# The next block's output product taken ahead of the last channel group of a feed-forward, with the residual sums passed through DRAM

## The chip, the cores and the metric

One NeuronCore of a Trainium2 chip. The metric is the device time of one execution in microseconds, given as the median of several runs.

## The reference

One layer of a decoder trunk over 2048 tokens of width 1024, in float32:

```python
h = rmsnorm(x, norm1_g) * (1 + sc1) + sh1
p = h @ w_in                                   # 27 columns of 128 channels
y = concat([rglru(...), hgrn2(...), rwkv7(...)]) * mix_beta   # three recurrent mixers over the tokens
x = x + g1 * (y @ w_out)
h = rmsnorm(x, norm2_g) * (1 + sc2) + sh2
x = x + g2 * ((silu(h @ w_gate) * (h @ w_up)) @ w_down)       # 2816 channels
return rmsnorm(x, final_g)
```

The six shift, scale and gate vectors come from a conditioning vector. The mixers carry a state from token to token; everything else works on each token alone.

## The kernel before

All tensors lie transposed, channels on the 128 partitions and tokens along the free axis. The tokens are cut into NB = 4 blocks of TB = 512, the width into KC = 8 pieces of 128, the feed-forward channels into NF = 22 groups of 128. So a block of x is eight tiles of 128x512.

Every projection runs in `project`: for each piece of the contraction three matmuls of 128x512, since both operands are split into a rounded part and a remainder (`hh`, `hl` of the activations, `wh`, `wl` of the weights): `hh` by `wh`, `hl` by `wh`, `hh` by `wl`. One product of a whole contraction of 1024 is 24 matmuls into one PSUM bank of the pool `pd`, which has three. A weight tile comes by a DMA of SyncE into a buffer `wr` (three of them), ScalarE rounds it to `wh` and VectorE forms `wl` (four of each). The pools `hh` and `hl` have 16 tiles each, the pool `xs` of plain float32 tiles 12.

A block b goes through these steps:

- `load_y(b)`: eight loads from the DRAM tensor `yd`, into which the mixers wrote, and their splits.
- `w_out_products(b)`: eight products of 24 matmuls. Each bank is evicted by one VectorE instruction (`stt`) that multiplies by the gate and adds to the tile of x; squares are summed on the side.
- `rstd_of`: the sums over the channels by four matmuls (L358 to L361), then logarithm and exponential on ScalarE. `make_h` (norm2) follows: for each of eight pieces a VectorE product with rstd (`xs<-xs,Q,rstd`), a ScalarE rounding (`hh<-xs,Q`) and a VectorE remainder (`hl<-xs,Q,hh`).
- `ffn(b)`: for each of the 22 channel groups two products of 24 matmuls (`ffn_up`); after every fourth group the eight products with `w_down` over those four groups (12 matmuls each, the last time over two groups, 6 matmuls each). Each is evicted by an `stt` that adds it to the tiles of x. So the groups go 4, 4, 4, 4, 4, 2. `load_y(b+1)` stands ahead of the w_down products of the last 4.
- `final_norm`: another `rstd_of` and eight `stt`, then the stores to `out`. For block b it stands behind the first product of `w_out_products(b+1)`.

Ahead of all this come the products with `w_in` for all blocks, whose results go to a DRAM tensor `pd` (stores of L1012). For the blocks 2 and 3 the last NT = 5 columns are done at the end, block 2 first, then block 3, then `load_y(0)`.

The mixers of all blocks are traced in small steps in between (`tick`, `step`, `finish`), so their instructions lie between the matmuls of the projections until they have done all four blocks.

What sets the order: a scheduler orders the instructions of each engine ahead of the run, by readiness in its own estimate and by a priority, which `level` sets. Lowest numbers go first: "out" (evictions) ahead of everything, then plain loads, "feed", "mix", and "dense" last. On the chip each engine runs its list in that order. SyncE's list holds nearly all DMAs; an entry that waits holds up those behind it.

Line 69 is the line of a wrapper through which all VectorE and ScalarE instructions go, so groups are told apart by their operands. L155 is the load of a weight tile, L164 that of any other tile, L267 the matmuls of `project`, L298 and L303 those of the mixers.

Of the kernel before, what the change touches and what calls it, by code (L numbers as in the profile page):

```python
# [10 lines left out]
F = mybir.dt.float32  # L11
# [3 lines left out]
OP = mybir.AluOpType  # L15
PSUM = bass.MemoryType.PSUM

T = 2048
D = 1024
FF = 2816  # L20
TB = 512
KC = D // 128
NB = T // TB
NF = FF // 128
# [11 lines left out]
IN_ORDER = (25, 26, 19, 16, 20, 17, 22, 23, 7, 4, 10, 13, 0, 2, 21, 18, 24, 8, 5, 11, 14, 1, 3, 9, 6, 12, 15)  # L36
# [38 lines left out]
def hybrid_kernel(ctx, tc, x, par, ada_w, w_in, rgw, igw, w_up, a_up, g_up, w_out,  # L75
                  w_gate, w_upf, w_down, cst, msk, out):
    nc = tc.nc
    G, PE, SP = nc.gpsimd, nc.tensor, nc.sync
# [3 lines left out]
    dp = ctx.enter_context(tc.tile_pool(name="dp", bufs=1))  # L82
# [7 lines left out]
    @contextmanager  # L90
    def level(name):

        clock[levels[-1]] = tc.cur_priority
        levels.append(name)
        tc.cur_priority = clock[name]
        yield
        clock[name] = tc.cur_priority
        levels.pop()
        tc.cur_priority = clock[levels[-1]]
# [4 lines left out]
    def stt(o, a, s, b, op0, op1):  # L104
        return V.scalar_tensor_tensor(o, a, s, b, op0=op0, op1=op1)
# [38 lines left out]
    def pc(name, i=0):  # L144
        a, b = PCOLS[name]
        assert a + i < b
        return P[:, a + i:a + i + 1]
# [98 lines left out]
    def load_w(src, fn):  # L246
        ws = []
        with level("load"):
            for c in range(0, src.shape[1], TB):
                n = min(TB, src.shape[1] - c)  # L250
                w = raw_w(src[:, c:c + n])
                hi, lo = w_parts()
                fn(w[:, :n], hi[:, :n], lo[:, :n])
                ws.append((hi, lo))
        return ws

    def project(h, *cols):

        ps = [bank("pd", 3) for ws in cols]
        tot = 3 * len(h)  # L260
        with level("dense"):
            for k, (hh, hl) in enumerate(h):
                c = slice((k % 4) * 128, (k % 4 + 1) * 128)
                for p, ws in zip(ps, cols):
                    wh, wl = ws[k // 4]
                    for n, (a, b) in enumerate(((wh, hh), (wh, hl), (wl, hh)), 3 * k):
                        PE.matmul(p, a[:, c], b, start=(n == 0), stop=(n == tot - 1))  # L267
                    now[0] += 0.68
                if k % (4 // len(ps)) == 4 // len(ps) - 1 or k == len(h) - 1:
                    tick()  # L270
        return ps
# [61 lines left out]
    def square_sum(s, t, k, tile=None, n=1):  # L333

        s, *last = s or (None,)
        if len(last) == n:
            if s is None:
                s = last.pop(0)
            else:
                V.tensor_add(s, s, last.pop(0))  # L340
        q = (tile or xs_)()
        if k == KC - 1:
            V.tensor_mul(q, t, t)
        else:
            squared[:] = [act(q, t, AF.Square)]
        return s, *last, q
# [18 lines left out]
    def load_x(src, b, k, tile=None):  # L365
        t = (tile or xs_)()
        load(t, src[k, :, b * TB:(b + 1) * TB])
        return t
# [15 lines left out]
    def make_h(xt, rs, gain, shift, table=None, ks=range(KC), over=True):  # L384

        hs = []

        def low(k, t, hi, lo):
            stt(lo, t, shift[:, k:k + 1], hi.bitcast(F), OP.add, OP.subtract)
            hs.append((hi, lo))  # L390

        todo = []
        for k in ks:
            x_ = xt(k)
            t = x_ if over else xs_()
            stt(t, x_, gain[:, k:k + 1], rs, OP.mult, OP.mult)
            hi, lo = parts_()
            i = act(hi, t, AF.Identity, bias=shift[:, k:k + 1])
            todo.append((k, t, hi, lo))
            if len(todo) > 2:  # L400
                low(*todo.pop(0))
        for a in todo:
            low(*a)
        if table is not None:
            order(A.preload_act_table_set(table), i)
        return hs

    def drain(it):
        for _ in it:
            pass  # L410
# [586 lines left out]
    def w_in_products(h, cols, side):  # L997

        n = 0
        while n < len(cols):  # L1000

            cs_ = cols[n:n + 2] if n == 0 and len(h) == 1 else cols[n:n + 1]
            ws = [W.pop(c) if c in W else load_w(w_in[c], split_v) for c in cs_]
            for i, b in enumerate(h):
                for j, (c, p) in enumerate(zip(cs_, project(h[b], *ws))):
                    with level("feed"):
                        t = xs_()
                        if (n + i + j) % 2:
                            act(t, p)
                        else:  # L1010
                            V.tensor_copy(t, p)
                        SP.dma_start(pd[c, :, b * TB:(b + 1) * TB], t)  # L1012
                        stored.add((c, b))
                    next(side, None)
            n += len(cs_)
# [24 lines left out]
    def load_y(b):  # L1040
        finish(b)
        ys = []
        for k in range(KC):
            t = load_x(yd, b, k)
            y = parts_()
            split_v(t, *y)
            ys.append(y)
        return ys

    def w_out_products(b, ys, before):  # L1050
        x1, s = [], None
        for d in range(KC):
            ws = load_w(w_out[d], split_v)
            t = load_x(x, b, d)
            p, = project(ys, ws)
            with level("out"):
                stt(t, p, G1[:, d:d + 1], t, OP.mult, OP.add)
            if d == 0:
                before()
            s = square_sum(s, t, d)  # L1060
            x1.append(t)
        return x1, rstd_of(s)

    def ffn_up(h, f):
        if f:
            p, = project(h, load_w(w_gate[f], split_v))
        else:
            p, pu = project(h, load_w(w_gate[f], split_v), load_w(w_upf[f], split_v))
        t = xs_()
        with level("out"):  # L1070
            act(t, p, AF.Silu)
        if f:
            pu, = project(h, load_w(w_upf[f], split_v))
        with level("out"):
            V.tensor_mul(t, pu, t)
        g = parts_()
        split_v(t, *g)
        return g

    def ffn(b, x1, rs):  # L1080
        h = make_h(lambda k: x1[k], rs, A2, B2, "silu_and_others", over=False)
        gs, s, ys = [], None, None
        for f0 in range(0, NF, 4):
            n = min(4, NF - f0)
            while len(gs) < min(f0 + n + (2 if f0 + n + 2 >= NF else 1), NF):
                gs.append(ffn_up(h, len(gs)))
            if len(gs) == NF and ys is None and b + 1 < NB:
                ys = load_y(b + 1)
            for d in range(KC):
                p, = project(gs[f0:f0 + n], load_w(w_down[d][:, f0 * 128:(f0 + n) * 128], split_v))  # L1090
                with level("out"):
                    stt(x1[d], p, G2[:, d:d + 1], x1[d], OP.mult, OP.add)
                if f0 + n == NF:
                    s = square_sum(s, x1[d], d, n=1 if b + 1 < NB else 2)

        def final_norm():
            rs = rstd_of(s)
            for d in range(KC):
                with level("dense"):
                    stt(x1[d], x1[d], pc("final_g", d), rs, OP.mult, OP.mult)  # L1100
                    SP.dma_start(out[d, :, b * TB:(b + 1) * TB], x1[d])

        return ys, final_norm

    side = ada_rest()
    NH, NT = 4, 5
    for b0 in range(0, NB, 2):
        h = {b0: h0}
        if b0 + 1 < NB:
            head, rest = IN_ORDER[:NH], IN_ORDER[NH:-NT]  # L1110
            w_in_products(h, head, ahead)
            drain(ahead)
            h1 = {b0 + 1: norm1(b0 + 1)}
            w_in_products(h1, head, side)
            h.update(h1)
            ahead = x_stats(range(b0 + 2, min(b0 + 4, NB)), 1)
            w_in_products(h, rest, chain(islice(side, 16), ahead, side))
            drain(ahead)
            w_in_products({b0: h[b0]}, IN_ORDER[-NT:], side)
            if b0 + 2 < NB:  # L1120
                h0 = norm1(b0 + 2)
            w_in_products(h1, IN_ORDER[-NT:], side)
        else:
            w_in_products(h, IN_ORDER, side)
    drain(side)
    with level("feed"):
        ys, before = load_y(0), lambda: None
    for b in range(NB):
        with level("feed"):
            ys, before = ffn(b, *w_out_products(b, ys, before))  # L1130
    before()


# [54 lines left out]
```

## Time and profile before

| | |
|---|---|
| Median of 3 runs | 2843.93 us (2843.27 to 2844.93) |
| The profiled execution: time, span | 2842.49 us, 2840.7 us |
| Mean granted TensorE clock | 0.989 |
| TensorE busy | 2724.8 us, 96% of the span |
| VectorE busy | 1934.6 us, 68% |
| ScalarE busy | 1472.7 us, 52% |
| DMA engines, mean | 124 GB/s, 352.27 MB moved |

The span runs from the first to the last instruction of the profiled execution; 1.8 us lie around it. In rows of groups the names of buffers stand without numbers, the count behind an x, the busy time in us, the mean time of one in ns, and after the second bar the idle time of the engine just before such instructions and what ended most of it.

### The profile page before, as it was taken

The numbers are of one execution on the slowest core, as the hardware profiler recorded it, in microseconds if no ns is written. First come the engines' busy times: TensorE is split into PE (matmuls) and PEld (weight loads), VectorE is DVE, ScalarE is ACT, GpSimd is POOL, SyncE is SP. The second block draws the span as 40 slices with busy tenths as digits, with TensorE's granted clock in tenths as the row PEclk, the third lists the DMA queues.
The fourth block names the chain that finished last, engine by engine and source line by source line (L and its number), as shares of the span: only waits on it lengthen the run. The fifth ranks groups of instructions, "written<-read, shape, count | busy, mean of one in ns | idle before, by whom it ended". The sixth has DMA issues, their size and how long they took to land. (4 is left out here: it accounts for less than half of the span.)

```text
span 2840.7 us, 41245 instructions
## 1 busy us (share of the span) xinstructions
PE 2724.8 (96%) x14842; PEld 2188.8 (77%) x14842; DVE 1934.6 (68%) x4150; ACT 1472.7 (52%) x2464; POOL 26.5 (1%) x29
## 2 busy tenths in 40 slices
PE   7999998999999999999999999999999999999998
PEld 6777776777877788877777877877777788788886
DVE  7668667866686785687887767788786445644445
ACT  5433854454647743666487546655863433533333
POOL 1000000000000000000000000000000000000000
PEclk9999999999999999999999999999999999999999
DMA  7553455544444242434533424335233334433332
GB/s 259 179 156 115 132 169 163 160 133 149 128 127 142 84 123 85 133 106 128 154 93 101 119 83 136 111 118 160 82 103 106 89 97 119 146 97 98 97 97 86
DMA packets 242588, 352.27 MB, mean 124 GB/s; under 512 B 72912, under 2 KB 78544, under 8 KB 242384
## 3 DMA queue, kind: packets, MB, share of 16 engines
q1 hardware_dynamic: 160144, 285.55, 32.4%
q10 hardware_dynamic: 82240, 64.09, 8.5%
q8 instruction: 117, 1.92, 0.3%
q14 instruction: 87, 0.71, 0.1%
HBM read 293.92 MB, written 55.62 MB: 123 GB/s over the span
## 5 line engine op out<-in xcount | busy, mean ns | idle before, releaser
L267 PE MATMUL pd<-hh,wh 128*128 128x512 f32 x3232 | 1289.5, 400 | 20.6 <-ACT hh L69 19.2
L267 PE MATMUL pd<-hl,wh 128*128 128x512 f32 x3232 | 1280.8, 396 | 3.8 <-DVE hl L69 3.7
L267 PE MATMUL pd<-hh,wl 128*128 128x512 f32 x3232 | 1281.9, 397 | 0.0
L69 ACT ACTIVATE wh<-wr 128x512 fp32r<-128x512 f32 (+1 forms) x752 | 463.8, 620 | 879.4 <-PE pd L267 692.9
L267 PEld LDWEIGHTS pd<-hh,wh 128*128 128x128 f32 x3232 | 612.2, 190 | 150.0 <-ACT hh L69 21.9
L267 PEld LDWEIGHTS pd<-hl,wh 128*128 128x128 f32 x3232 | 612.3, 189 | 133.8 <-DVE hl L69 9.1
L267 PEld LDWEIGHTS pd<-hh,wl 128*128 128x128 f32 x3232 | 611.8, 189 | 127.9 <-issue 3.4
L69 DVE TENSOR_TENSOR wl<-wr,wh 128x512 fp32r<-128x512 f32 (+1 forms) x752 | 504.2, 674 | 301.1 <-ACT wh L69 284.2
L69 ACT ACT_TABLE_LOAD x225 | 288.7, 1283 | 12.0 <-DVE th L69 4.5
L69 DVE SCALAR_TENSOR_TENSOR xs<-pd,Q,xs 128x512 f32<-128x512 f32 x224 | 167.6, 748 | 131.5 <-PE pd L267 123.5
L69 DVE TENSOR_TENSOR th<-th 128x256 f32<-128x256 f32 (+7 forms) x355 | 158.0, 458 | 26.8 <-ACT th L69 23.4
L69 ACT ACTIVATE th<-th 128x512 f32<-128x512 f32 (+2 forms) x153 | 93.5, 612 | 47.5 <-DVE th L69 22.8
L69 DVE TENSOR_TENSOR big<-big 128x30 f32<-128x30 f32 (+7 forms) x480 | 108.2, 225 | 10.1 <-DMA big<-nd 0.2
L69 DVE TENSOR_TENSOR xs<-pd,xs 128x512 f32<-128x512 f32 x88 | 60.6, 689 | 76.8 <-PE pd L267 74.2
L69 ACT ACTIVATE xs<-pd 128x512 f32<-128x512 f32 x140 | 82.6, 590 | 57.0 <-PE pd L267 53.0
L69 ACT ACTIVATE hh<-xs 128x512 fp32r<-128x512 f32 x120 | 74.4, 628 | 39.8 <-DVE xs L69 25.0
L69 DVE TENSOR_TENSOR hl<-xs,hh 128x512 fp32r<-128x512 f32 x120 | 81.7, 688 | 14.1 <-ACT hh L69 9.8
L69 ACT ACTIVATE hw<-big,we 64x64 f32<-64x64 f32 x192 | 66.2, 345 | 37.9 <-DVE big L69 31.6
L69 ACT ACTIVATE tr<-tr 128x512 fp32r<-128x512 f32 (+4 forms) x112 | 69.5, 627 | 17.5 <-DVE tr L69 16.3
L69 ACT ACTIVATE xs<-xs 128x512 f32<-128x512 f32 x77 | 48.1, 627 | 43.6 <-DVE xs L69 40.1
L69 DVE SCALAR_TENSOR_TENSOR big<-pc,we,hw 64x64 f32<-64x64 f32 x168 | 47.5, 283 | 30.8 <-PE pc L298 28.1
L69 DVE TENSOR_TENSOR tr<-tr 128x512 fp32r<-128x512 f32 (+2 forms) x80 | 54.7, 686 | 19.1 <-ACT tr L69 18.5
(183 smaller groups left out, 2220.4 us busy)
## 6 DMA issues: line engine op xcount, KB each, us to landing
wr<-in_w_gate SPq DMA_DIRECT2D x176, 256.0 KB, 2.6
wr<-in_w_upf SPq DMA_DIRECT2D x176, 256.0 KB, 2.6
wr<-in_w_down SPq DMA_DIRECT2D x160, 256.0 KB, 2.7
wr<-in_w_in SPq DMA_DIRECT2D x144, 256.0 KB, 3.3
pd<-xs SPq DMA_DIRECT2D x108, 256.0 KB, 3.1
xs<-in_x SPq DMA_DIRECT2D x72, 256.0 KB, 4.3
wr<-in_ada_w SPq DMA_DIRECT2D x64, 256.0 KB, 3.2
th<-pd ACTq DMA_DIRECT2D x64, 256.0 KB, 3.5
```

The source lines that it names most:

```text
L69: return f(*a, **k)
L267: PE.matmul(p, a[:, c], b, start=(n == 0), stop=(n == tot - 1))
```

## The change

Four things, all in the order of the work. The matmuls, evictions and splits stay as many as they were.

1. The groups of a feed-forward go 2, 4, 4, 4, 4, 4.
2. `ffn` does all groups but the last. Then `load_y(b+1)`, `w_out_products(b+1)` and norm2 of b+1 follow, and only then `ffn_last(b)`, the w_down products of the last four groups of block b.
3. Two blocks' sums are alive at once, and the pool `xs` has no room for both. So in the fifth group the tiles of block b are stored to a DRAM tensor `xr`; `ffn_last` loads them into tiles of the pools `hh` and `hl` (`spare`), adds its products and stores them to `xf`; `final_norm` loads them from `xf`, again into such tiles, and stands behind the channel groups 0 to 2 of the next feed-forward. Block 3 does without this.
4. The five last w_in columns of block 3 (5 products of 24 matmuls) go from ahead of `load_y(0)` to behind norm2 of block 0.

So there are 96 more DMAs of 256 KB: for each of three blocks 8 stores to `xr`, 8 loads from it, 8 stores to `xf`, 8 loads from it.

```diff
-    def ffn(b, x1, rs):
-        h = make_h(lambda k: x1[k], rs, A2, B2, "silu_and_others", over=False)
...
+    GROUPS = (2, 4, 4, 4, 4, 4)
+    def ffn_down(gs, f0, d):
+        p, = project(gs, load_w(w_down[d][:, f0 * 128:(f0 + len(gs)) * 128], split_v))
+        return p
+    def norm2(x1, rs):
+        return make_h(lambda k: x1[k], rs, A2, B2, "silu_and_others", over=False)
+    def ffn(b, x1, h, before):
+        gs, f0 = [], 0
+        for i, n in enumerate(GROUPS[:-1]):
+            while len(gs) < min(f0 + n + 1, NF):
+                gs.append(ffn_up(h, len(gs)))
+            if i == 0:
+                before()
+            if i == len(GROUPS) - 2:
+                while len(gs) < NF:
+                    gs.append(ffn_up(h, len(gs)))
             for d in range(KC):
+                p = ffn_down(gs[f0:f0 + n], f0, d)
                 with level("out"):
                     stt(x1[d], p, G2[:, d:d + 1], x1[d], OP.mult, OP.add)
+                    if b + 1 < NB and i == len(GROUPS) - 2:
+                        SP.dma_start(xr[d, :, b * TB:(b + 1) * TB], x1[d])
+            f0 += n
+        return gs[f0:], f0
+    def spare(i):
+        return dp.tile([128, TB], F, name="hl" if i % 2 else "hh", bufs=16)
+    def ffn_last(b, x1, gs, f0):
+        s, ts_ = None, []
+        for d in range(KC):
+            t = load_x(xr, b, d, lambda: spare(d)) if b + 1 < NB else x1[d]
+            p = ffn_down(gs, f0, d)
+            with level("out"):
+                stt(t, p, G2[:, d:d + 1], t, OP.mult, OP.add)
+                if b + 1 < NB:
+                    SP.dma_start(xf[d, :, b * TB:(b + 1) * TB], t)
+            s = square_sum(s, t, d, n=1 if b + 1 < NB else 2)
         def final_norm():
             rs = rstd_of(s)
             for d in range(KC):
+                with level("feed"):
+                    t = load_x(xf, b, d, lambda: spare(d)) if b + 1 < NB else x1[d]
                 with level("dense"):
-                    stt(x1[d], x1[d], pc("final_g", d), rs, OP.mult, OP.mult)
-                    SP.dma_start(out[d, :, b * TB:(b + 1) * TB], x1[d])
+                    stt(t, t, pc("final_g", d), rs, OP.mult, OP.mult)
+                    SP.dma_start(out[d, :, b * TB:(b + 1) * TB], t)
...
     with level("feed"):
-        ys, before = load_y(0), lambda: None
-    for b in range(NB):
-        with level("feed"):
-            ys, before = ffn(b, *w_out_products(b, ys, before))
+        x1, rs = w_out_products(0, load_y(0))
+        h = norm2(x1, rs)
+        w_in_products(h1, IN_ORDER[-NT:], side)
+        before = lambda: None
+        for b in range(NB):
+            gs, f0 = ffn(b, x1, h, before)
+            if b + 1 < NB:
+                x1, rs = w_out_products(b + 1, load_y(b + 1))
+                h = norm2(x1, rs)
+            before = ffn_last(b, x1, gs, f0)
     before()
```

The order of VectorE at the norm2 of block 3, before. The rows with rstd and `hl<-xs,Q_79,hh` are the end of norm2, `xs<-pd,xs` is the eviction of the first `ffn_up`, `wl<-wr,wh` are splits of weights:

```order
L69 SCALAR_TENSOR_TENSOR xs<-xs,Q_79,rstd 128x512
L69 SCALAR_TENSOR_TENSOR hl<-xs,Q_79,hh 128x512
L69 TENSOR_TENSOR wl<-wr,wh 128x512 x2
L69 SCALAR_TENSOR_TENSOR hl<-xs,Q_79,hh 128x512 x2
L69 TENSOR_TENSOR wl<-wr,wh 128x512
L69 TENSOR_TENSOR xs<-pd,xs 128x512
```

So the next instruction behind norm2 that frees a bank was that of the feed-forward's first product. The same place on VectorE now. `hh<-pd,Q_79,hh` and `hl<-pd,Q_79,hl` are the evictions of `ffn_last(2)` into the spare tiles; TensorE does these products behind w_out(3):

```order
L69 SCALAR_TENSOR_TENSOR hl<-xs,Q_79,hh 128x512
L69 SCALAR_TENSOR_TENSOR xs<-xs,Q_79,rstd 128x512
L69 SCALAR_TENSOR_TENSOR hl<-xs,Q_79,hh 128x512 x3
L69 SCALAR_TENSOR_TENSOR hh<-pd,Q_79,hh 128x512 x2
L69 SCALAR_TENSOR_TENSOR hl<-pd,Q_79,hl 128x512
L69 TENSOR_TENSOR xs<-xs 128x512 x2
L69 SCALAR_TENSOR_TENSOR hl<-pd,Q_79,hl 128x512
L69 TENSOR_TENSOR wl<-wr,wh 128x512
```

Behind norm2, where the eviction of an `ffn_up` stood, now stand the evictions of the w_down products, the first of them behind all sixteen instructions of norm2.

SyncE at the same place now (before, only loads of w_out, w_gate, w_upf and x stood there): the loads of the sums come behind those of eight w_down tiles and two of w_gate.

```order
L164 DMA xs<-in_x 128x512
L155 DMA wr<-in_w_down 128x512 x5
L155 DMA wr<-in_w_gate 128x512 x2
L164 DMA hh<-xr 128x512 x2
L164 DMA hl<-xr 128x512 x2
L164 DMA hh<-xr 128x512
L1122 DMA xf<-hh 128x512 x2
L1122 DMA xf<-hl 128x512
L164 DMA hl<-xr 128x512
```

On SyncE the sums' way through DRAM has been put between the weights of this product and those of the next feed-forward.

VectorE at the norm2 of block 0 now. `xs<-pd` are evictions of the moved w_in columns:

```order
L69 SCALAR_TENSOR_TENSOR xs<-xs,Q_79,rstd 128x512
L69 SCALAR_TENSOR_TENSOR hl<-xs,Q_79,hh 128x512
L69 TENSOR_TENSOR wl<-wr,wh 128x512
L69 SCALAR_TENSOR_TENSOR hl<-xs,Q_79,hh 128x512 x2
L69 COPY xs<-pd 128x512
L69 TENSOR_TENSOR wl<-wr,wh 128x512
L69 COPY xs<-pd 128x512
```

There too, the first eviction of the product that now follows the output product stands behind norm2.

More of the change, by code (lines that the diff above doesn't have):

```diff
@@ L1048, in load_y, with w_out_products @@
         return ys
-    def w_out_products(b, ys, before):
+    def w_out_products(b, ys):
         x1, s = [], None
@@ L1057, in w_out_products @@
                 stt(t, p, G1[:, d:d + 1], t, OP.mult, OP.add)
-            if d == 0:
-                before()
             s = square_sum(s, t, d)
@@ L1078, in ffn_up @@
         return g
-    def ffn(b, x1, rs):
-        h = make_h(lambda k: x1[k], rs, A2, B2, "silu_and_others", over=False)
[L1082 to L1085, printed above, removed]
-                gs.append(ffn_up(h, len(gs)))
-            if len(gs) == NF and ys is None and b + 1 < NB:
-                ys = load_y(b + 1)
+    xr = tc.dram_tile([KC, 128, T], F, name="xr")
+    xf = tc.dram_tile([KC, 128, T], F, name="xf")
+    GROUPS = (2, 4, 4, 4, 4, 4)
[8 more added lines that the diff above has]
+            while len(gs) < min(f0 + n + 1, NF):
+                gs.append(ffn_up(h, len(gs)))
+            if i == 0:
[3 more added lines that the diff above has]
+                    gs.append(ffn_up(h, len(gs)))
             for d in range(KC):
-                p, = project(gs[f0:f0 + n], load_w(w_down[d][:, f0 * 128:(f0 + n) * 128], split_v))
+                p = ffn_down(gs[f0:f0 + n], f0, d)
                 with level("out"):
                     stt(x1[d], p, G2[:, d:d + 1], x1[d], OP.mult, OP.add)
-                if f0 + n == NF:
-                    s = square_sum(s, x1[d], d, n=1 if b + 1 < NB else 2)
+                    if b + 1 < NB and i == len(GROUPS) - 2:
[14 more added lines that the diff above has]
+            s = square_sum(s, t, d, n=1 if b + 1 < NB else 2)
         def final_norm():
@@ L1098, in final_norm @@
             for d in range(KC):
+                with level("feed"):
+                    t = load_x(xf, b, d, lambda: spare(d)) if b + 1 < NB else x1[d]
                 with level("dense"):
-                    stt(x1[d], x1[d], pc("final_g", d), rs, OP.mult, OP.mult)
-                    SP.dma_start(out[d, :, b * TB:(b + 1) * TB], x1[d])
-        return ys, final_norm
+                    stt(t, t, pc("final_g", d), rs, OP.mult, OP.mult)
+                    SP.dma_start(out[d, :, b * TB:(b + 1) * TB], t)
+        return final_norm
     side = ada_rest()
@@ L1121, in hybrid_kernel @@
                 h0 = norm1(b0 + 2)
-            w_in_products(h1, IN_ORDER[-NT:], side)
-        else:
-            w_in_products(h, IN_ORDER, side)
+                w_in_products(h1, IN_ORDER[-NT:], side)
     drain(side)
     with level("feed"):
-        ys, before = load_y(0), lambda: None
-    for b in range(NB):
-        with level("feed"):
-            ys, before = ffn(b, *w_out_products(b, ys, before))
+        x1, rs = w_out_products(0, load_y(0))
+        h = norm2(x1, rs)
+        w_in_products(h1, IN_ORDER[-NT:], side)
+        before = lambda: None
[5 more added lines that the diff above has]
+            before = ffn_last(b, x1, gs, f0)
     before()
```

## Prediction

> **What bounds the kernel now.** I read the page first, for the engine that carries the end, then the waits of TensorE, then stretches of the time line where those waits lie.
>
> ```profile
> PE 2724.8 (96%) x14842; PEld 2188.8 (77%) x14842; DVE 1934.6 (68%) x4150; ACT 1472.7 (52%) x2464; POOL 26.5 (1%) x29
> PE pd L267 <- ACT hh L69: 19.2, 6, 5.0
> PE pd L361 <- DVE xs L69: 4.4, 3, 2.0
> PE pd L267 <- DVE hl L69: 3.7, 4, 1.9
> ```
>
> TensorE is the bound: busy 2724.8 of 2840.7 us. The three rows of waits (total, times, longest) are what an output product and its norm cost: the sum of squares, then `hh` and `hl` of norm2. Together 27.3 us in four blocks. Idle PE time elsewhere belongs to the mixers and the start, which the change leaves alone. So all that can be won is about 27 us and what the clock loses. The stretches of these places:
>
> ```profile
> core 0: us, PE busy (x) PEld busy (x) DVE busy (x) ACT busy (x) POOL busy (x), PEclk, DMA share, GB/s
> 858.50:871.50 13.00, 8.75 (x30) 6.32 (x30) 7.35 (x14) 11.68 (x21) 0.00 (x0) 0.74 0.64 208
> 938.00:954.00 16.00, 11.78 (x122) 7.62 (x121) 14.08 (x26) 12.01 (x17) 0.00 (x0) 0.79 0.19 60
> 1443.50:1458.00 14.50, 10.13 (x39) 6.28 (x39) 13.77 (x26) 11.52 (x19) 0.00 (x0) 1.00 0.10 33
> 1979.00:1991.00 12.00, 6.78 (x29) 4.06 (x29) 11.55 (x25) 9.10 (x15) 0.00 (x0) 1.00 0.21 75
> 2456.70:2469.00 12.30, 6.46 (x16) 3.75 (x15) 8.64 (x13) 7.15 (x10) 0.00 (x0) 0.72 0.23 72
> 2464.00:2468.00 4.00, 3.94 (x8) 2.65 (x9) 4.00 (x7) 2.77 (x4) 0.00 (x0) 0.50 0.00 0
> ```
>
> The first row is the start of w_out(0), the next four are the norm2 of blocks 0 to 3, the last is the first work behind the wait of block 3, at a granted clock of 0.50. Block 3 has no mixers and shows the chain bare:
>
> ```profile
> 2456.23 0.40 PE L267 MATMUL pd<-hh,wh 128*128 128x512 f32 x1
> 2456.47 0.39 PE L267 MATMUL pd<-hl,wh 128*128 128x512 f32 x1
> 2456.70 0.40 PE L267 MATMUL pd<-hh,wl 128*128 128x512 f32 x1
> 2457.13 0.75 DVE L69 SCALAR_TENSOR_TENSOR xs<-pd,Q,xs 128x512 f32<-128x512 f32 x1 [0.88 <-PE pd L267]
> 2458.66 1.12 PE L361 MATMUL pd<-xs,aones 128*128 128x512 f32 x2 [1.57 <-DVE xs L69]
> 2459.83 0.69 ACT L69 ACTIVATE rstd<-pd,epsc 128x512 f32<-128x512 f32 x1 [1.25 <-PE pd L361]
> 2461.82 0.63 ACT L69 ACTIVATE rstd<-rstd 128x512 f32<-128x512 f32 x1
> 2462.49 2.08 DVE L69 SCALAR_TENSOR_TENSOR xs<-xs,Q,rstd 128x512 f32<-128x512 f32 x3 [3.19 <-ACT rstd L69]
> 2464.05 1.22 PE L267 MATMUL pd<-hh,wh 128*128 128x512 f32 x2 [4.26 <-ACT hh L69]
> 2471.11 0.74 DVE L69 SCALAR_TENSOR_TENSOR hl<-xs,Q,hh 128x512 fp32r<-128x512 f32 x1
> 2471.89 1.37 DVE L69 TENSOR_TENSOR wl<-wr,wh 128x512 fp32r<-128x512 f32 x2
> 2473.18 1.41 DVE L69 SCALAR_TENSOR_TENSOR hl<-xs,Q,hh 128x512 fp32r<-128x512 f32 x2
> ```
>
> Matmuls issue 0.23 us apart (2456.23, 2456.47, 2456.70), so the output product ends its issue at 2456.93. rstd is there at 2462.45, 5.5 us on; norm2 then keeps VectorE busy from 2462.49 to 2474.59, 12.1 us, two weight splits in it. But TensorE starts again at 2464.05, as soon as the first `hh` is there, and follows VectorE piece by piece. Keep these two numbers apart: norm2 is 12 us long, TensorE waits for far less.
>
> **The change part by part.** Losses before: block 3 fills 12.3 us with 16 matmuls of 0.23, so 12.3 - 3.7 = 8.6 lost. Block 1 is idle for 14.5 - 10.1 = 4.4, block 2 for 5.2; a record is 0.40 long at a pitch of 0.23, so every gap hides some 0.2 and I take 5.5 and 6.0. Block 0: 4.2 idle, plus a fifth of 16 us at the clock of 0.79, 3.4: 7.6.
>
> *Blocks 1 to 3: the last w_down products move behind w_out.* TensorE has 8 products of 12 matmuls, 2.73 us each, that need neither rstd nor norm2. They would cover 21.9 us, if their banks were emptied. There are three banks. Products 0, 1 and 2 take 3 x 2.73 = 8.2, with L361 in between (two matmuls, 0.46) 8.7 us. Product 3 needs the bank of product 0, emptied by the first `hh<-pd,Q_79,hh`, which the order puts on VectorE behind all sixteen instructions of norm2. Those cannot start before rstd. So: rstd at 6.0 (5.5, and up to a microsecond more where L361 now waits behind 8 to 12 matmuls of product 0), norm2 and two or three splits 12.1, the eviction
>
> ```profile
> L69 DVE SCALAR_TENSOR_TENSOR xs<-pd,Q,xs 128x512 f32<-128x512 f32 x224 | 167.6, 748 | 131.5 <-PE pd L267 123.5
> L69 DVE TENSOR_TENSOR wl<-wr,wh 128x512 fp32r<-128x512 f32 (+1 forms) x752 | 504.2, 674 | 301.1 <-ACT wh L69 284.2
> ```
>
> of 0.75: bank 0 is free 18.9 us after the output product. TensorE, done at 8.7, stands for 10.2 us. What was a wait for the first piece of norm2 has become a wait for its end.
>
> The clock belongs to it. Block 3 waited 4.26 us in one piece and then worked 4 us and more at 0.50; blocks 1 and 2, whose waits the mixers' matmuls broke up, kept 1.00. A wait of 10.2 in one piece is nearest to block 3: about 4.2 us of work at half speed, 2.1 lost. So 12.3 lost at each of the three, against 5.5, 6.0 and 8.6: +6.8, +6.3, +3.7. The Trainium skill speaks against the change here ("TensorE: Matmul & The Clock Gate", What's actually happening): a matrix unit idle for a window of about 3.4 us falls to half clock, and needs as long a busy one to come back. The trace agrees, 4.26 us of idling and 0.50 after it; by the page's window the loss would be an estimated 1.7 each instead of 2.1, 1.2 us less in all. Without any clock loss in blocks 1 and 2, as now, 4.2 less.
>
> VectorE might be thought to let the eviction pass. Its rows stand in the trace in the order of the program, waits included. The same page says that VectorE and ScalarE are strict FIFO (Architectural detail); no run here shows otherwise.
>
> *The loads from `xr`* stand on SyncE behind w_down and w_gate loads that wait for `wr` buffers. A `wr` is free when its split is done, and that needs one of four `wl`, which product 2 gives back at 8.7. The split itself stands inside norm2 on VectorE, so the loads go out at some 12 us and
>
> ```profile
> xs<-in_x SPq DMA_DIRECT2D x72, 256.0 KB, 4.3
> xs<-yd SPq DMA_DIRECT2D x32, 256.0 KB, 3.9
> pd<-xs SPq DMA_DIRECT2D x108, 256.0 KB, 3.1
> ```
>
> by the rows of such loads land 3.9 to 4.3 later, at 16: too late for 8.7, but ahead of 18.9. Cost behind the VectorE order: 0; if five of them in a row take double, 1.5 us each.
>
> *Block 0: five w_in products behind norm2*, 120 matmuls or 27 us. The first eviction (`xs<-pd` on VectorE) is again behind norm2, about 20 to 21 us after the output product (three to four splits stand inside). But three banks of 24 matmuls hold 16.4 us, with L361 and the mixers' matmuls 18 to 19. I take 2 us of wait left of 7.6: -5.6. Ends: -7.6 if VectorE is quick, -3 with the clock down.
>
> *The start of w_out(0).* The row 858.50 has 13.0 us, clock 0.74. The loads of y wait on SyncE behind a store:
>
> ```profile
> 860.17 0.33 SPq L1012 DMA_DIRECT2D pd<-xs  x1
> 860.54 0.43 SPq L164 DMA_DIRECT2D xs<-yd  x1
> 862.38 3.06 SPq L164 DMA_DIRECT2D xs<-yd  x6
> ```
>
> The changed order has a w_in product and its store there too, only that of block 2. 0, within 2 either way.
>
> *The first group of two instead of the last*: the same products and splits, 0. *Stores to `xr` and `xf`, loads for `final_norm`, `out`*: 96 DMAs of 256 KB, 25 MB more than 352, on DMA engines used at 124 GB/s; not the bandwidth, but SyncE's order. The stores of `out` now stand between loads of w_gate and w_upf and each waits for a VectorE instruction of lowest priority. Before, they stood between w_out loads in the same way. Cover: three `wr` and four `wh`, so several loads of 2.7 us of matmuls each lie ahead. I take 0, at worst 3 us a block. *The last norm*: its inputs are the same, 0.
>
> Sum: 6.8 + 6.3 + 3.7 - 5.6 = +11.2. Against the profiled execution 2842.5 + 11.2 = 2853.7; the median of the runs lies 1.4 above that execution, so 2855.
>
> **The rivals.**
>
> *The norm is hidden as the order of TensorE would have it.* If the evictions didn't hold up product 3, the losses of all four norms would go: 7.6 + 5.5 + 6.0 + 8.6 = 27.7, so 2816. For it: 21.9 us of products against 7 to 8 us up to the first `hh`. Against it: three banks and the order of VectorE. It decides from the point at which bank 0 is free by 8.7. A half of it, the eviction in the middle of norm2, would give 2830 to 2836. Chance together 0.18.
>
> *The wait is there, but small things shrink it.* Mixers' matmuls break up the wait in blocks 1 and 2 so that the clock holds (-4.2), and block 0 is won in full (-2): 2849. The loads, not VectorE, would give much the same: landing at 16 makes 16.8 - 8.7 = 8.1 us. Change within the bound: chance 0.22.
>
> *SyncE holds up weights*: with 3 us a block for `out` and `xf` and 1.5 for the loads, 2855 + 3 x 4.5 = 2868. For it: all of these pass through one queue that waits in order. Against: the depth of the weights' buffers. Chance 0.15.
>
> **How the numbers follow.** A measurement of this kernel can tell about 0.2%, 5.7 us, from no change, so 2849.6 and 2838.2 are the bounds. My forecast has 0.45, the slow rival 0.15: slower 0.60. Within it 0.22, faster 0.18. The likeliest case alone spans 2850 to 2860. The range goes up to the slow rival, 2868, and down to 2836, which takes in the second rival and leaves out most of the first.
>
> **What would show it.** In the profile after: at each of the blocks 1 to 3 one wait of TensorE (L267, bank `pd`) of some 10 us, released by a VectorE `hh<-pd,Q,hh`; a clock of about 0.5 for 4 us behind it; the waits for ACT `hh` and DVE `hl` all but gone; the first `hh<-pd` behind the last `hl<-xs,Q,hh`. In block 0 a wait of about 2 us for an eviction. Wrong I would be if product 3 starts within 9 us of the output product, if TensorE waits in the feed-forward for `wh` or `wl`, or if w_out of the next block starts late for want of y.

## The result: slower by 39.6 us

The changed kernel takes 2884.01 us (median of 4 runs, 2882.07 to 2890.26) against 2844.43 before: a ratio of 1.0138, interval 1.0126 to 1.0151, or +39.6 us. The forecast was slower, 2855, with 2836 to 2868 as the range. The sign came as forecast, the size lies outside the range. One of the four runs before took 9339.66 us; without it their median is 2843.93. The profiled execution of the changed kernel has a span of 2888.5 us and took 2890.26, 6.3 more than the median.

The profile after, first the page and then the waits of TensorE (total, times, longest):

```profile
PE 2743.7 (95%) x14842; PEld 2202.3 (76%) x14842; DVE 1934.5 (67%) x4150; ACT 1502.6 (52%) x2485; POOL 26.5 (1%) x29
```

```profile
PE pd L267 <- DVE hh L69: 31.5, 3, 11.6
PE ph L298 <- DVE th L69: 20.8, 14, 4.4
PE pd L267 <- ACT hh L69: 6.1, 2, 3.4
PE pd L267 <- DVE hl L69: 3.4, 3, 2.7
PE pd L361 <- DVE xs L69: 1.6, 1, 1.6
```

The rows of the old waits (19.2 + 4.4 + 3.7 = 27.3) are down to 11.1. Of the 27.3, only 13.0 stood at the four norms, by the time line; these are gone, and the 11.1 stand elsewhere. In their place stand three waits of 31.5 us together, each for a VectorE instruction that writes an `hh` from a bank: the eviction of the moved products. Beyond that, TensorE is busy for 18.9 us more with the same 14842 matmuls (the mean granted clock is 0.979, before it was 0.989), and ScalarE for 30 us more. The clock was in the forecast with 6.3 us, ScalarE's time with nothing.

The boundary to block 3, without mixers, from the time line: TensorE, VectorE, SyncE.

```profile
2476.78 0.39 PE L267 MATMUL pd<-hh,wl 128*128 128x512 f32 x1
2477.00 0.39 PE L267 MATMUL pd<-hh,wh 128*128 128x512 f32 x1
2478.82 1.04 PE L361 MATMUL pd<-xs,aones 128*128 128x512 f32 x2
2495.77 0.79 PE L267 MATMUL pd<-hh,wh 128*128 128x512 f32 x1 [9.52 <-DVE hh L69]
```

```profile
2482.56 0.75 DVE L69 SCALAR_TENSOR_TENSOR xs<-xs,Q,rstd 128x512 f32<-128x512 f32 x1 [3.27 <-ACT rstd L69]
...
2492.99 2.07 DVE L69 SCALAR_TENSOR_TENSOR hl<-xs,Q,hh 128x512 fp32r<-128x512 f32 x3
2494.98 1.40 DVE L69 SCALAR_TENSOR_TENSOR hh<-pd,Q,hh 128x512 f32<-128x512 f32 x2
```

```profile
2485.21 3.58 SPq L155 DMA_DIRECT2D wr<-in_w_gate  x2
2489.20 0.80 SPq L164 DMA_DIRECT2D hh<-xr  x2
```

```profile
DMA to landing us min/median/max: 4.7/4.7/4.7
```

The output product's issue ends at 2477.0. rstd is there at 2482.56, 5.6 us on. Norm2 fills VectorE up to 2495.06, the eviction follows without a gap, and product 3 starts at 2495.77: 18.8 us after the output product, where 18.9 was forecast. The first load from `xr` goes out 12.2 us after the output product and lands 4.7 us later (the last row, for this load alone), at 2493.9. That is 1.2 us ahead of the end of norm2. At the two boundaries before, the first load lands 0.7 us behind the end of norm2 (block 1) and some 0.4 ahead of it (block 2). So both causes end close together: had VectorE been free, the sums would hardly have been there earlier.

The clock at the three boundaries, and for the 5 us behind each of the three waits:

```profile
core 0: us, PE busy (x) PEld busy (x) DVE busy (x) ACT busy (x) POOL busy (x), PEclk, DMA share, GB/s
1419.80:1461.50 41.70, 29.99 (x132) 23.47 (x130) 37.80 (x69) 26.06 (x39) 0.00 (x0) 0.84 0.56 166
1979.90:2019.70 39.80, 28.63 (x119) 22.13 (x119) 36.06 (x62) 25.74 (x36) 0.00 (x0) 0.87 0.54 162
2477.00:2512.20 35.20, 25.68 (x99) 20.20 (x98) 26.07 (x39) 18.71 (x27) 0.00 (x0) 0.85 0.60 183
1441.60:1446.60 5.00, 5.00 (x13) 3.75 (x14) 4.96 (x10) 1.78 (x3) 0.00 (x0) 0.50 0.77 210
2001.70:2006.70 5.00, 5.00 (x12) 3.75 (x13) 4.87 (x9) 1.78 (x3) 0.00 (x0) 0.50 0.79 218
2495.80:2500.80 5.00, 5.00 (x12) 3.94 (x13) 2.62 (x4) 1.78 (x3) 0.00 (x0) 0.50 0.86 209
```

In each row stand the length of the stretch, the busy time of each engine, and after POOL the granted clock (PEclk). The first three stretches run from the start of the moved products to their end. TensorE idles 11.7, 11.2 and 9.5 us in them, and its clock falls to 0.50 behind the wait in the blocks with mixers too: twelve matmuls in the 5.0 us of the last row, at 0.23 they would take 2.8.

Of ScalarE's 30 us, 27 are loads of function tables (`ACT_TABLE_LOAD`, 1.28 us each), 225 in the kernel before and 246 in the changed one. With the activation Silu left out, further down, there are 182.

```profile
L69 ACT ACT_TABLE_LOAD x225 | 288.7, 1283 | 12.0 <-DVE th L69 4.5
```

```profile
L69 ACT ACT_TABLE_LOAD x246 | 315.6, 1283 | 13.8 <-DVE pcar L69 4.2
```

### The profile page after: what moved, and what is told of

It is laid out like the page before. It is cut to its first block, busy times and chain, and to the rows that moved or that the text cites. A ratio compares the mean times of both kernels' runs of the same rounds, so it can differ in the third digit from the quotient of the medians.

```text
span 2888.5 us, 41384 instructions
## 1 busy us (share of the span) xinstructions
PE 2743.7 (95%) x14842; PEld 2202.3 (76%) x14842; DVE 1934.5 (67%) x4150; ACT 1502.6 (52%) x2485; POOL 26.5 (1%) x29
## 4 chain that ended last, share of the span: by engine, by line
PE 42%; DVE 5%; ACT 4%; DMA 2%; issue 1%; ACTq 0%; DVEq 0%; SPq 0%
PE pd L267 36%; PE pm L298 2%; PE ph L298 2%; PE pc L298 1%; DVE xs L69 1%; ACT L69 1%; DVE wl L69 1%; ACT wh L69 1%; DVE big L69 1%; DVE hl L69 1%; ACT th L69 1%; DMA th<-pd 1%; ACT tr L69 0%; DMA wr<-in_w_gate 0%; DVE tr L69 0%
## 5 line engine op out<-in xcount | busy, mean ns | idle before, releaser
L267 PE MATMUL pd<-hh,wh 128*128 128x512 f32 x3232 | 1299.4, 403 | 41.4 <-DVE hh L69 31.5
L69 DVE SCALAR_TENSOR_TENSOR xs<-pd,Q,xs 128x512 f32<-128x512 f32 x200 | 149.7, 748 | 113.5 <-PE pd L267 112.0
L69 DVE TENSOR_TENSOR th<-th 128x256 f32<-128x256 f32 (+5 forms) x355 | 158.2, 458 | 29.3 <-ACT th L69 23.8
L69 DVE SCALAR_TENSOR_TENSOR big<-pc,we,hw 64x64 f32<-64x64 f32 x168 | 47.5, 283 | 23.5 <-PE pc L298 19.9
L69 DVE SCALAR_TENSOR_TENSOR big<-big,th,ph 64x64 f32<-64x64 f32 x168 | 46.9, 279 | 22.2 <-PE ph L298 18.7
```

Of the source, the lines that this page charges most:

```text
L69: return f(*a, **k)
```

## The experiments

Times are medians; the kernel before, run beside each, took 2843.5 to 2844.3 us.

**The loads of the sums, written earlier.**

```diff
+    early = []
     def w_out_products(b, ys):
         for d in range(KC):
+            if b and d == 0:
+                early[:] = [load_x(xr, b - 1, k, lambda: spare(k)) for k in range(KC)]
...
-            t = load_x(xr, b, d, lambda: spare(d)) if b + 1 < NB else x1[d]
+            t = early[d] if b + 1 < NB else x1[d]
```

> The changed kernel, but the eight loads from xr of a boundary are written ahead of the first product of w_out instead of one by one inside ffn_last. The order then has the evictions of ffn_last's products 0 and 1 ahead of, and the others between, the instructions of norm2. Theory W (wake): the three waits for an eviction (31.5 us) and all that came behind them, the mixers' longer waits and the half clock, are one thing; then all of the 39.6 us go and the covered norms show: 2815 to 2830. Theory M (mixers): only the 31.5 us and about 6 of clock go, the rest (some 25 us of mixers' waits and clock in the feed-forwards) comes from how the mixers' steps are laid between the moved products and stays: 2838 to 2850. If SyncE or the eviction order was not the cause: 2880.

2834.41 us against 2844.09 before, 0.9966 (0.9953 to 0.9979): 49.6 us below the changed kernel, and 9.7 below the kernel before. The three waits have gone from TensorE. Its time at the boundaries, and VectorE at the last of them:

```profile
1410.70:1434.30 23.60, 23.60 (x105) 19.07 (x104) 20.95 (x37) 18.91 (x26) 0.00 (x0) 1.00 0.54 173
1950.00:1977.00 27.00, 27.00 (x211) 21.72 (x210) 22.88 (x36) 16.09 (x27) 0.00 (x0) 1.00 0.58 168
2431.30:2454.00 22.70, 22.70 (x99) 18.32 (x99) 19.92 (x31) 12.38 (x19) 0.00 (x0) 1.00 0.60 185
```

```profile
2435.17 0.75 DVE L69 SCALAR_TENSOR_TENSOR hh<-pd,Q,hh 128x512 f32<-128x512 f32 x1 [1.48 <-PE pd L267]
2436.90 0.75 DVE L69 SCALAR_TENSOR_TENSOR xs<-xs,Q,rstd 128x512 f32<-128x512 f32 x1 [0.98 <-ACT rstd L69]
2437.57 0.69 DVE L69 TENSOR_TENSOR wl<-wr,wh 128x512 fp32r<-128x512 f32 x1
2438.17 0.75 DVE L69 SCALAR_TENSOR_TENSOR hl<-pd,Q,hl 128x512 f32<-128x512 f32 x1
```

TensorE is busy without a gap, at full clock. The first eviction now stands ahead of norm2 and the others between its instructions. Nothing was said about VectorE in the edit: the scheduler put the evictions there when it expected the sums in time. The time lies between the two theories' ranges: more went than the waits and their clock, and less than all that the norms had lost was won. Why less is read further down, from TensorE's idle time between the norms.

**The w_in columns alone.** The kernel before with

```diff
         h = make_h(lambda k: x1[k], rs, A2, B2, "silu_and_others", over=False)
+        if b == 0:
+            w_in_products(h1, IN_ORDER[-NT:], side)
...
             if b0 + 2 < NB:
                 h0 = norm1(b0 + 2)
-            w_in_products(h1, IN_ORDER[-NT:], side)
+                w_in_products(h1, IN_ORDER[-NT:], side)
```

> The kernel before with only the five w_in columns of block 3 moved behind norm2 of block 0. The prediction's term: -5.6, that is 2838. Theory W: the same, since nothing else is touched. Theory M: the moved columns also shift the mixers' steps against the projections in the feed-forward of block 0, which lost 5 us more in the changed kernel: 2840 to 2846.

2839.55, 0.9982 (0.9972 to 0.9992): -4.5, forecast -5.6. The remaining wait for an eviction in block 0, forecast at 2 us, is 1.0:

```profile
PE pd L267 <- DVE xs L69: 1.0, 1, 1.0
```

**The changed kernel without that move.** The five columns stand ahead of `load_y(0)` again.

> The changed kernel with those five columns back ahead of load_y(0). Theory W: slower than the changed kernel by what the columns win, 2884 + 4 to 6 = 2888 to 2890; the waits for evictions at the three boundaries remain, some 10 us each. Theory M: the mixers' waits are laid anew, so anything from 2870 to 2890.

2887.27, 1.0147 (1.0124 to 1.0171), 3.3 above the changed kernel; the intervals overlap. The three waits for evictions are again 31.5 us.

**The groups alone.** The kernel before with

```diff
-        for f0 in range(0, NF, 4):
-            n = min(4, NF - f0)
-            while len(gs) < min(f0 + n + (2 if f0 + n + 2 >= NF else 1), NF):
+        for f0, n in ((0, 2), (2, 4), (6, 4), (10, 4), (14, 4), (18, 4)):
+            while len(gs) < (NF if f0 == 14 else min(f0 + n + 1, NF)):
```

> The kernel before with the channel groups 2, 4, 4, 4, 4, 4 and nothing else (the y loads ahead of the fifth group). The prediction's term: 0, so 2844. Theory W: 2842 to 2846. Theory M: the steps of the mixers lie elsewhere, up to 10 us either way.

2858.08 against 2844.09, 1.0048 (1.0031 to 1.0066): +14.0 where the forecast had 0. TensorE's matmuls are the same and block 3 takes as long as before; the time goes in the blocks 1 and 2 (9.0 and 5.2 us more from one norm2 to the next, in block 0 it is 3.3 less). ScalarE has 16 table loads more:

```profile
L69 ACT ACT_TABLE_LOAD x241 | 309.2, 1283 | 13.5 <-DVE tr L69 2.2 <-DVE pcar L69 1.8 <-DMA xd<-big 1.5
```

The trace doesn't show that TensorE waits for them: between two norms it idles 22.0 us in all, before it was 21.4. It shows a change at norm2 of the blocks 1 and 2. The rows are 24 us around each of these norms, first before, then with the groups alone:

```profile
1442.00:1466.00 24.00, 19.62 (x88) 13.70 (x88) 21.37 (x42) 19.42 (x32) 0.00 (x0) 1.00 0.19 61
1978.00:2002.00 24.00, 18.78 (x90) 13.66 (x89) 22.47 (x45) 19.76 (x34) 0.00 (x0) 1.00 0.21 74
```

```profile
1439.00:1463.00 24.00, 16.44 (x61) 12.01 (x61) 20.32 (x36) 13.46 (x19) 0.00 (x0) 0.86 0.28 89
1984.00:2008.00 24.00, 18.51 (x69) 13.12 (x70) 21.70 (x40) 15.93 (x22) 0.00 (x0) 0.79 0.24 77
```

TensorE idles 7.6 and 5.5 us there instead of 4.4 and 5.2, and the clock, 1.00 before, is 0.86 and 0.79. Before, 36 and 41 matmuls of the mixers (L298) lay in these stretches and broke up the waits; with the other groups 8 and 18 do.

**The y tiles loaded straight into hl.**

```diff
-            t = load_x(yd, b, k)
             y = parts_()
+            t = load_x(yd, b, k, lambda: y[1].bitcast(F))
             split_v(t, *y)
```

> The changed kernel, but the y tiles are loaded straight into their hl tiles (ScalarE rounds them to hh, VectorE subtracts in place), so they need no xs tile that waits for a store to xr. The late reload of the sums stays. In the changed kernel ScalarE waited 24.1 us for loads of yd (14.1 before), and a mixer's matmul waited 4.4 us behind that in block 0. Theory Y (ScalarE held up by late y loads delays the mixers): some 10 us of the mixers' waits go, 2870 to 2878. Theory W (all of it is the wait for the evictions and its wake): 2882 to 2886.

2876.47, 1.0109 (1.0089 to 1.0128): 7.5 below the changed kernel, inside the range of theory Y. But its reason isn't in the trace. ScalarE's waits for these loads, in the changed kernel and in this run:

```profile
ACT hh L69 <- DMA xs<-yd: 24.1, 17, 3.0
```

```profile
ACT hh L69 <- DMA hl<-yd: 35.0, 24, 2.8
```

They grew. TensorE waits less for the mixers' `th` on VectorE (the row of 20.8 has 15.0), but all its waits together are 130.3 us, in the changed kernel 130.4. Theory Y falls as it was stated; why the edit wins 7.5 us is open.

> Early reload of the sums and y tiles loaded straight into hl tiles, together. Theory Y: 8 to 12 us below the early reload alone, 2822 to 2827. Theory W: as the early reload alone, 2831 to 2837.

Both edits together: 2835.18, 0.9967 (0.9951 to 0.9983), the same as the early reload alone. Late y loads aren't what keeps that kernel from more.

**W_out ahead at the last boundary alone**, with early reload: blocks 0 and 1 as before, the moved columns kept.

```diff
+    AHEAD = {2}
...
+        groups = (2, 4, 4, 4, 4) if b in AHEAD else (4, 4, 4, 4, 4)
+                if b not in AHEAD and b + 1 < NB:
+                    ys = load_y(b + 1)
...
+            if b in AHEAD:
+                x0, (x1, rs) = x1, w_out_products(b + 1, load_y(b + 1))
+                h = norm2(x1, rs)
+                before = ffn_last(b, x0, gs, f0)
+            else:
+                before = ffn_last(b, x1, gs, f0)
+                if b + 1 < NB:
+                    x1, rs = w_out_products(b + 1, ys, before)
```

> The moved w_in columns, and w_out ahead with early reload at the last boundary alone (blocks 2 to 3), where the mixers have ended; blocks 0 and 1 go as in the kernel before, groups 4, 4, 4, 4, 4, 2. If the norm itself is hidden by the early reload and the rest of the changed kernel's loss belongs to the mixers' blocks: 2844 - 4.5 for the columns - 8 for the norm of block 3 = 2831 to 2832, and block 3 shows no wait over 1 us. If the trip through DRAM or the groups of two cost by themselves: 2836 to 2840.

2829.04, 0.9944 (0.9925 to 0.9964): 15 us below before, the fastest of the kernels with Silu, and 5.4 below the early reload at all three boundaries (the intervals of these two overlap). The norm of block 3 is hidden, with the trip through DRAM and all:

```profile
2433.50:2456.20 22.70, 22.70 (x99) 18.33 (x99) 19.85 (x31) 12.38 (x20) 0.00 (x0) 1.00 0.59 185
2456.20:2480.00 23.80, 23.80 (x106) 19.71 (x105) 15.30 (x25) 12.83 (x21) 0.00 (x0) 1.00 0.37 116
```

The first row is the eight moved products, the second the feed-forward behind them: no gap, clock 1.00.

> As the run with w_out ahead at the last boundary alone (2829), but with the groups 4, 4, 4, 4, 4, 2 in block 2 as well, so that two groups instead of four are left to cover the norm: eight products of 6 matmuls, 10.9 us instead of 21.8, against 7.1 us from the output product to the first hh. If cover is all that matters: the same 2829, up to 2 us more because norm2 ends after the cover. If the groups of two first cost in block 2 through the mixers: 2825 to 2828.

With `groups = (4, 4, 4, 4, 4)` in block 2 too, two channel groups are left over: 2836.17, 0.9971 (0.9955 to 0.9988), 7.1 slower, though the intervals overlap. At most 2 was expected. More cover was needed than the first `hh`:

```profile
2439.80:2451.50 11.70, 11.70 (x51) 9.28 (x50) 9.62 (x17) 5.79 (x10) 0.00 (x0) 1.00 0.64 190
2451.50:2480.00 28.50, 24.98 (x97) 19.73 (x97) 22.42 (x35) 17.39 (x28) 0.00 (x0) 0.88 0.39 132
```

The cover ends 11.7 us in; behind it TensorE idles 3.5 us (2.0 for a `wh`, 1.5 for an `hl`, none for an `hh`) and the mean clock falls to 0.88, where it was 1.00 with four groups.

> With Silu. As the run with w_out ahead at the last boundary alone (2829, 231 table loads), but at the boundary from block 1 to 2 as well, with early reload (238 table loads). If moving w_out in a block with mixers wins the norm it covers: 2822 to 2826. If the gain is taken back by the mixers: 2829 to 2836.

`AHEAD = {1, 2}`: 2835.27, 0.9963 (0.9949 to 0.9977), 6.2 above the last boundary alone (the intervals overlap here too). In a block with mixers the move wins nothing, even with the reload early: TensorE idles 4.6 us less at the four norms and 7.7 more between them.

**Stores on GpSimd.** Early reload and y straight into hl, the stores to `xr`, `xf` and `out` by `G.dma_start`.

> Early reload, y straight into hl, and the stores to xr, xf and out issued by GpSimd instead of SyncE. If stores that wait on SyncE ahead of weight loads hold up the weights (ScalarE waited 12.4 and 7.5 us for w_gate and w_upf in the changed kernel, 0 and 1.4 before): 3 to 10 us below the same kernel with the stores on SyncE. If that wait is not on the path: the same within 3 us.

2871.79, 1.009 (1.0071 to 1.011): 36.6 slower than the same kernel with SyncE. This falsifies neither reading of SyncE's queue, since the new queue is slower by itself. The stores at the end of the kernel, on GpSimd and, in the run with SyncE, all eight in one row:

```profile
2846.74 0.56 POOL L1136 DMA_DIRECT2D out<-xs  x1 [298.77 <-DVE xs L69]
2849.35 0.54 POOL L1136 DMA_DIRECT2D out<-xs  x1 [2.06 <-DVE xs L69]
...
2865.26 0.54 POOL L1136 DMA_DIRECT2D out<-xs  x1 [2.09 <-issue]
```

```profile
2823.50 4.97 SPq L1136 DMA_DIRECT2D out<-xs  x8
```

2.65 us apart (18.5 over seven) against 0.62 (4.97 over eight).

**Silu left out**, in four kernels: a plain copy in its place and no table preload for it, so that all have 182 or 183 table loads.

```diff
-            act(t, p, AF.Silu)
+            act(t, p, AF.Identity)
```

> The kernel before with the activation Silu of the feed-forward left out (a plain copy in its place), so that ScalarE changes its function table 182 times instead of 225. It is the base of the next two. Both theories: faster than before where the mixers' steps wait for ScalarE, 2825 to 2844.

> The groups 2, 4, 4, 4, 4, 4 alone, Silu left out as in the run above; 182 table loads here too, where with Silu it was 241 against 225. Theory T (tables): the 13.7 us that the groups cost come from 16 table loads more, laid between the mixers' steps on ScalarE, so here they go: within 4 us of the base. Theory M (how the mixers' steps lie between the products): they stay, +8 to +14 on the base.

> The changed kernel, Silu left out as in the two runs above, 182 table loads instead of 246. The evictions of the w_down products stand behind norm2 as in the changed kernel, so three waits of some 10 us remain. Theory T: what is left is the prediction's sum, +8 to +18 on the base without Silu. Theory M: +30 to +42 on it, as with Silu.

> The early reload with Silu left out (183 table loads instead of 244), to be set beside the kernel before and the changed kernel without Silu (2848 and 2853). The three waits for evictions are gone from it. If the losses of the norms in the mixers' blocks come back as mixers' waits only because of the table loads, all that was to be hidden shows here: 2848 - 4.5 for the columns - some 20 = 2820 to 2828. If they come back whatever the tables (the mixers' own chains fill the gap): 2832 to 2840. Taken from the changed kernel without Silu: its three waits with the clock behind them, 38 us by the profile, would go in full in the first case, and about half of them in the second.

| kernel | with Silu, us | table loads | without, us | table loads |
|---|---|---|---|---|
| before | 2844.1 | 225 | 2848.2 | 182 |
| groups alone | 2858.1 | 241 | 2848.1 | 182 |
| changed | 2884.0 | 246 | 2852.5 | 182 |
| early reload | 2834.4 | 244 | 2827.9 | 183 |

Ratios to the kernel before, with Silu in it: 1.0017 (0.9999 to 1.0034), 1.0014 (0.9999 to 1.003), 1.0019 (1.0004 to 1.0034), 0.9933 (0.9912 to 0.9954). Without Silu the groups cost nothing, and the whole change 4.3 us instead of 39.6. The waits are still in that kernel: one shows as the eviction, the other two come out under mixers' matmuls which stand in TensorE's queue there (the waits of 8.5 and 8.0).

```profile
PE ph L298 <- DVE th L69: 15.9, 11, 8.5
PE pd L267 <- DVE hh L69: 9.5, 1, 9.5
PE pc L298 <- ACT big L69: 8.6, 3, 8.0
```

By the numbers that it named, theory T is borne out for the groups, and for the change it even overshot: +4.3, under the +8 to +18 expected. But the comparison doesn't single out the table loads. The kernel before got no faster when 43 loads went, and its trace without Silu shows why the groups cost nothing there: at norm2 of the blocks 1 and 2 this kernel, with 18 matmuls of the mixers in each stretch, has now lost the clock as well.

```profile
1451.00:1475.00 24.00, 18.48 (x75) 14.05 (x74) 19.91 (x34) 20.90 (x32) 0.00 (x0) 0.86 0.25 81
1988.00:2012.00 24.00, 16.91 (x67) 12.27 (x66) 18.88 (x33) 22.28 (x32) 0.00 (x0) 0.86 0.20 68
```

Leaving Silu out lays the mixers' steps anew; whether the loads' own time or the order that goes with them costs the microseconds is not shown. Early reload without Silu reaches 2827.9, at the edge of the range for "what was to be hidden can be hidden": 20.4 below its base, where with Silu it was 9.7.

## Why the prediction was wrong

Set one behind the other, the runs with Silu give: the groups +14.0 (2858.1 - 2844.1); from there to the early reload -23.7 (2834.4 - 2858.1); from there to the changed kernel +49.6. The forecast had 0, -25.7 (5.6 for the columns, 5.5 + 6.0 + 8.6 for the norms) and +36.9 (three times 12.3). That the three steps add up to 39.9 proves nothing, since each starts where the one before it ends. Where the time lies is read from the traces. The table has TensorE's idle time, the length of a stretch less PE's busy time, in stretches of two kinds: 24 us around each of the four norm2, from 4 us ahead of its L361 to 20 us behind, and the three stretches from there to the next. Each of these three holds a block's feed-forward and the next w_out; where the five w_in columns are moved, they stand in the first.

| kernel | around the four norm2, us | between them, us |
|---|---|---|
| before | 19.6 | 21.4 |
| columns alone | 16.4 | 22.6 |
| groups alone | 23.1 | 22.0 |
| changed | 33.6 | 41.3 |
| early reload | 1.3 | 39.7 |
| w_out ahead at the last boundary alone | 10.1 | 22.8 |
| the same and from block 1 to 2 | 5.5 | 30.5 |
| before, without Silu | 22.6 | 18.5 |
| changed, without Silu | 27.7 | 25.2 |
| early reload, without Silu | 1.7 | 30.8 |

Of the second kind, the stretch behind norm2 of block 1, before, changed, and with the early reload:

```profile
1466.00:1978.00 512.00, 502.16 (x2926) 399.74 (x2925) 392.76 (x884) 309.26 (x518) 5.68 (x6) 1.00 0.40 117
```

```profile
1442.00:1979.00 537.00, 517.03 (x2967) 410.79 (x2967) 394.07 (x894) 320.19 (x532) 5.67 (x6) 0.98 0.42 125
```

```profile
1433.00:1949.00 516.00, 494.59 (x2799) 394.09 (x2798) 388.84 (x884) 312.42 (x522) 5.68 (x6) 0.99 0.42 126
```

- **The wait in place of the wait: right.** 18.8 us from the output product to product 3 against 18.9; 31.5 us of waits for three evictions against 30.6; clock 0.50 behind each, in the blocks with mixers too, where the forecast chose block 3 as the nearest row. One edit that lets the evictions pass takes 49.6 us off, and the idle time at the norms falls from 33.6 to 1.3. The rule of the Trainium skill on an idle window ("TensorE: Matmul & The Clock Gate", What's actually happening) agrees with all three.
- **The columns: right.** -4.5 against -5.6, 1.0 us of wait left against 2.
- **"Idle PE time elsewhere belongs to the mixers and the start, which the change leaves alone": the step that failed.** The sum had no term for it. Between the norms TensorE idles 41.3 us in the changed kernel, 21.4 before: 19.9 more, and the waits of the mixers' matmuls (L298, L303) make up 39.3 and 19.6 of that. It is not the wake of the three waits, for with the early reload, which has none of them, it is 39.7. It comes with w_out ahead in a block in which the mixers still run: moved at the last boundary alone it leaves 22.8, and with the boundary from block 1 to 2 it is 30.5. What in the mixers' chains makes them wait is open. Without Silu the growth is smaller, 6.7 for the change and 12.3 for the early reload, so a part of it goes with Silu and a part does not.
- **"The first group of two instead of the last: the same products and splits, 0": missed as well, by 14.0.** The step counted matmuls, evictions and splits, and left out where the mixers' matmuls would then lie. The forecast itself had said that these keep the clock at 1.00 at norm2 of the blocks 1 and 2; with the groups alone it is 0.86 and 0.79. How much of the 14.0 this makes is not shown, nor whether it is still lost in the changed kernel, where other products follow w_out. That the 16 table loads more are the cause is not shown either.
- **The boundaries' +36.9.** In block 3, where the same 99 matmuls stand in both stretches, the term is right: 35.2 - 22.7 = 12.5 against 12.3. At the other two boundaries the stretches differ by 18.1 and 12.8 (41.7 - 23.6 and 39.8 - 27.0), but other matmuls of the mixers stand in them, so these are no prices. The rest of the 49.6 isn't located; it does not lie in the idle time between the norms.
- **The loads from `xr`: "cost behind the VectorE order: 0" was right, but narrowly.** They took 5.5 us in the median, not 3.9 to 4.3, and in block 1 the first one landed 0.7 us behind the end of norm2. The rival in which only the loads count, given as 8.1 us of wait, would have been some 9.
- **The reading of the waits before was too wide.** The 27.3 us were taken for the four norms, which had 13.0 of them; the rest stood in the w_in products and at the start of w_out(0). The sum doesn't use the 27.3.
- **The rival on SyncE's order** wasn't settled: its test put a slower queue in the place of the one in question.

## What to carry to other kernels

When products are moved ahead to cover a wait, follow what empties their PSUM banks: with three banks they cover three products, unless the evictions can run, and what these need (here a load written too late) decides where a scheduler puts them. Look for the cover up to the end of the covered work, not up to its first piece: 21.8 us of products hid the norm, 10.9 did not. And when the order of one stream of work changes, ask where a second stream that is interleaved with it will then wait, and which of the first one's waits it no longer breaks up: "the same work, 0" holds for neither. Try the edit first where nothing else is interleaved: the last boundary alone won 15 us with the columns, the others gave part of it back.

## What the runs showed of the hardware

Stores of 256 KB issued by GpSimd left it 2.65 us apart, those by SyncE 0.62 apart; eight of them stand at the end of this kernel. The time to land once issued is alike, 2.3 us (GpSimd) and 2.2 (SyncE) by the lists of DMAs.
